# Which 32 KB block of DRAM each SBUF partition holds: a map of 32 x 4 blocks, and the last store in one piece

## Chip, cores, metric

One core of one Trainium2 chip. The metric is device time in microseconds (us). Faster or slower needs 2%; smaller differences are given with their 95% interval.

## The reference

Rotary position embedding on x of shape [16, 512, 1024], float32, with 16 heads of 64 and tables cos and sin of [512, 32]:

```python
x = x.reshape(batch, seq, num_heads, head_dim)
x1, x2 = x[..., :half_dim], x[..., half_dim:]
cos = cos[None, :, None, :]
sin = sin[None, :, None, :]
rotated = np.concatenate([x1 * cos - x2 * sin, x1 * sin + x2 * cos], axis=-1)
```

33.55 MB go in and 33.55 MB come out; everything else is small.

## The kernel before

The tensor is cut into 8 slabs of 4 MB (two batch entries each). A slab is 128 blocks of 32 KB, 8 rows of 1024 floats each, and partition p holds block p. Loads are issued by SyncE, stores by ScalarE; five slab buffers go round, and a load waits for the store that frees its buffer.

```python
    def dram(t, s, a=0, n=W):
        return bass.AP(tensor=t.tensor, offset=t.offset + s * nb * seq * dim + a,
                       ap=[[W, P], [1, n]])
    ...
    def load(s):
        slab[s] = slabs.tile([P, W], f32, tag="slab", name="slab")
        return nc.sync.dma_start(out=slab[s], in_=dram(x, s))
```

The tables arrive in one layout (partition p: sequence positions 4p to 4p+3) and are spread to the slab's layout by matmuls with a 0/1 matrix `pick`, which GpSimd builds:

```python
    for g in range(2 * G):
        part = view(pick, g * P, (SP, P // SP), (1, SP))
        nc.gpsimd.affine_select(
            out=part, in_=part, compare_op=mybir.AluOpType.not_equal,
            fill=1.0 if g < G else -1.0, base=-(g % G),
            pattern=[[0, P // SP], [-G, SP]], channel_multiplier=1)
```

Each slab is cast to bfloat16 on ScalarE, goes through two multiplies and one add on VectorE, is cast back on ScalarE and stored. The last slab is handled and stored in two halves:

```python
        back = nc.scalar.copy(out=xs, in_=xu)
        if s == nslabs - 1:
            ...  # keep the second half's cast behind the first half's store
            part = nc.scalar.dma_start(
                out=dram(out_flat, s, r * dim, n * dim), in_=xs)
        elif r + n == rpp:
            nc.scalar.dma_start(out=dram(out_flat, s), in_=slab[s])
            if s + slots < nslabs:
                load(s + slots)
```

## Time and profile before

| | before |
|---|---|
| median of 4 runs | 162.49 us (162.31 to 162.63) |
| span of the profiled run | 160.4 us |
| VectorE, ScalarE busy | 108.5 us, 113.5 us |
| the two DMA queues' share of 16 engines | 49.4% + 48.5% |
| 32 KB packet, median | 1.213 us |

How to read it: the busiest compute engine works 71% of the time and the DMA engines nearly all of it. The prediction below shows these lines and works with them. It also uses single packet records, which no view of the profile prints: start, duration, size and queue of each DMA packet. They do not say which of the 16 engines moved it; so what is said of single engines is inferred. Two things read from them: the **first byte** (start of the first load packet, 1.77 us before) and the **tail** (from the last completion packet to the end of the span, 1.45 us before).

### The profile page before, as it was taken

The page shows a single profiled execution, that of the slowest core. Times are in us where ns is not written, and L with a number is a line of the kernel's source. Part 1 is how long each engine was busy: PE and PEld are TensorE (multiplying, and loading weights), DVE is VectorE, ACT ScalarE, POOL GpSimd, SP SyncE. Part 2 cuts the span into 40 slices and gives each one's busy share as a digit, 9 for nine tenths or more (in the row PEclk, how much of TensorE's full clock was granted, in tenths as well). Part 3 has the DMA queues.
Part 4 walks back from the last instruction along what each step waited for, and adds up shares of the span by engine and source line. Part 5 has one row for each costly group of instructions (what it writes and reads, how often), then busy time and mean ns, then how long its engine had stood idle before and what let it go on. Part 6 is the DMA issues. An engine that isn't in the chain of part 4 may idle for free.

```text
span 160.4 us, 169 instructions
## 1 busy us (share of the span) xinstructions
PE 1.0 (1%) x8; PEld 0.8 (1%) x8; DVE 108.5 (68%) x34; ACT 113.5 (71%) x23; POOL 3.4 (2%) x12
## 2 busy tenths in 40 slices
PE   0011000000000000000000000000000000000000
PEld 0010000000000000000000000000000000000000
DVE  0003799999989979997996099939649599920000
ACT  3006939998998999899907997099995999471000
POOL 7000000000000000000000000000000000000000
DMA  7999999999999999999999999999999999999994
GB/s 229 441 409 400 474 433 392 449 466 392 392 392 449 466 392 425 490 392 409 490 409 409 482 417 392 490 425 392 458 458 392 433 482 392 417 490 400 400 437 208
DMA packets 2512, 67.24 MB, mean 419 GB/s; under 512 B 304, under 2 KB 304, under 8 KB 336
## 3 DMA queue, kind: packets, MB, share of 16 engines
q1 hardware_dynamic: 1152, 33.55, 49.4%
q10 hardware_dynamic: 1296, 33.56, 48.5%
q0 software_dynamic: 64, 0.13, 0.2%
HBM read 33.69 MB, written 33.55 MB: 419 GB/s over the span
## 4 chain that ended last, share of the span: by engine, by line
DMA 59%; ACT 17%; issue 9%; DVE 4%; SPq 0%; POOLq 0%
DMA slab<-in_x_dram 40%; DMA out_dram<-slab 15%; ACT slab L146 11%; ACT xb L119 6%; DMA raw<-in_cos_dram 4%; DVE xb L143 1%; DVE xb L140 1%; DVE slab L140 1%; SPq L62 0%; POOLq L177 0%
## 5 line engine op out<-in xcount | busy, mean ns | idle before, releaser
L119 ACT CAST xb<-slab 128x4096 bf16<-128x4096 f32 (+1 forms) x11 | 56.6, 5155 | 27.4 <-DMA slab<-in_x_dram 26.1
L146 ACT CAST slab<-xb 128x4096 f32<-128x4096 bf16 (+1 forms) x11 | 56.6, 5153 | 3.4 <-DVE xb L143 3.4
L140 DVE TENSOR_TENSOR slab<-xb,tab 128x4096 bf16<-128x4096 bf16 (+1 forms) x11 | 35.9, 3260 | 19.7 <-ACT xb L119 19.6
L143 DVE TENSOR_TENSOR xb<-xb,slab 128x4096 bf16<-128x4096 bf16 (+1 forms) x11 | 35.9, 3261 | 0.3
L140 DVE TENSOR_TENSOR xb<-xb,tab 128x4096 bf16<-128x4096 bf16 (+1 forms) x11 | 35.9, 3260 | 0.3
L110 DVE CAST tab<-acc 128x1024 bf16<-128x1024 f32 x1 | 1.2, 1225 | 12.6 <-PE acc L104 12.6
L119 ACT ACT_TABLE_LOAD x1 | 1.3, 1283 | 0.7 <-PEq L177 0.7
L104 PE MATMUL acc<-tab,pick 128*128 128x128 bf16 x8 | 1.0, 305 | 11.6 <-POOL tab L98 11.6
L92 POOL TENSOR_SCALAR_AFFINE_SELECT pick<-pick 128x128 bf16<-128x128 bf16 x4 | 1.0, 289 | 0.1
L104 PEld LDWEIGHTS <-pick 128*128 128x128 bf16 x8 | 0.8, 136 | 11.4 <-issue 8.1
L73 POOL DMA_DIRECT2D raw<-in_cos_dram x1 | 0.7, 677 | 0.8 <-POOLq L177 0.8
L98 POOL CAST tab<-raw 128x256 bf16<-128x256 f32 x1 | 0.4, 398 | 7.0 <-DMA raw<-in_sin_dram 7.0
L89 POOL MEMSET pick<- 128x512 bf16 x1 | 0.5, 544 | 0.0
L73 POOL DMA_DIRECT2D raw<-in_sin_dram x1 | 0.5, 537 | 0.0
L177 POOL MEMSET const-float32-0.0<- 128x1 f32 x1 | 0.1, 99 | 0.2 <-issue 0.2
L177 POOL MEMSET const-bfloat16-1.0<- 128x1 bf16 x1 | 0.1, 102 | 0.0
L177 POOL MEMSET const-uint8-127<- 128x1 uint8 x1 | 0.1, 102 | 0.0
L177 POOL MEMSET const-float32-1.0<- 128x1 f32 x1 | 0.1, 99 | 0.0
## 6 DMA issues: line engine op xcount, KB each, us to landing
slab<-in_x_dram SPq DMA_DIRECT2D x8, 4096.0 KB, 24.6
out_dram<-slab ACTq DMA_DIRECT2D x7, 4096.0 KB, 27.8
out_dram<-slab ACTq DMA_DIRECT2D x2, 2048.0 KB, 15.3
raw<-in_cos_dram POOLq DMA_DIRECT2D x1, 64.0 KB, 7.1
raw<-in_sin_dram POOLq DMA_DIRECT2D x1, 64.0 KB, 9.1
```

The source lines that it names most:

```text
L73: table[i] = nc.gpsimd.dma_start(out=view(raw, i * TR * half, (1, TR * half)), in_=bass.AP(tensor=src.tensor, offset=src.offset, ap=[[TR * ...
L89: nc.gpsimd.memset(pick, 0.0)
L92: nc.gpsimd.affine_select(out=part, in_=part, compare_op=mybir.AluOpType.not_equal, fill=1.0 if g < G else -1.0, base=-(g % G), pattern=[[ ...
L98: nc.gpsimd.tensor_copy(out=tab1, in_=raw)
L104: nc.tensor.matmul(view(acc, (i * rpp + g * TR) * hd + h * half, (hd, TR), (1, half)), view(pick, (i * h * G + g) * P, (1, P)), view(tab1, ...
L110: nc.vector.tensor_copy(out=tab, in_=acc)
L119: nc.scalar.copy(out=view(xb[s], r * dim, (1, n * dim)), in_=view(slab[s], r * dim, (1, n * dim)))
L140: nc.vector.tensor_mul(out=t, in0=xu, in1=view(tab, a + r * hd, (hd, n), (0, nh), (1, hd)))
L143: nc.vector.tensor_add(out=xu, in0=xu, in1=view(t2, half, (hd, n * nh), (-half, 2), (1, half)))
L146: back = nc.scalar.copy(out=xs, in_=xu)
L177: nc = _bacc.Bacc("TRN2", target_bir_lowering=False, num_devices=1)
```

## The change

Partition 4i+j now holds block i+32j, where it held block 4i+j, so the DRAM side of a transfer is a pattern of 32 x 4 blocks where it was 128 plain rows. The intent was that the DMA engines work on neighbouring 32 KB blocks at any one time. The `pick` matrices follow the new map, and the last slab is stored whole.

```diff
-    def dram(t, s, a=0, n=W):
-        return bass.AP(tensor=t.tensor, offset=t.offset + s * nb * seq * dim + a,
-                       ap=[[W, P], [1, n]])
+    PJ = P // 4
+
+    def dram(t, s):
+        return bass.AP(tensor=t.tensor, offset=t.offset + s * nb * seq * dim,
+                       ap=[[W, PJ], [PJ * W, 4], [1, W]])
...
-        part = view(pick, g * P, (SP, P // SP), (1, SP))
+        part = view(pick, g * P, (4, PJ), (2, 2), (1, 2))
...
-            pattern=[[0, P // SP], [-G, SP]], channel_multiplier=1)
+            pattern=[[-G, PJ], [0, 2], [-G * PJ, 2]], channel_multiplier=1)
...
-        back = nc.scalar.copy(out=xs, in_=xu)
-        if s == nslabs - 1:
-            ...
-            part = nc.scalar.dma_start(
-                out=dram(out_flat, s, r * dim, n * dim), in_=xs)
-        elif r + n == rpp:
+        nc.scalar.copy(out=xs, in_=xu)
+        if r + n == rpp:
             nc.scalar.dma_start(out=dram(out_flat, s), in_=slab[s])
```

More of the change, by code (lines that the diff above doesn't have):

```diff
@@ L34 @@
     W = rpp * dim
-    SP = seq // rpp
     TW = rpp * half
@@ L144 @@
             out=xu, in0=xu, in1=view(t2, half, (hd, n * nh), (-half, 2), (1, half)))
-        back = nc.scalar.copy(out=xs, in_=xu)
-        if s == nslabs - 1:
-            if r > 0:
-                tc.add_manual_dep(
-                    back.ins, part.ins.name,
-                    mybir.DependencyInfo(mybir.DependencyClass.NoSync,
-                                         mybir.DependencyReason.DATA),
-                    reason="issue")
-            part = nc.scalar.dma_start(
-                out=dram(out_flat, s, r * dim, n * dim), in_=xs)
-        elif r + n == rpp:
+        nc.scalar.copy(out=xs, in_=xu)
+        if r + n == rpp:
             nc.scalar.dma_start(out=dram(out_flat, s), in_=slab[s])
```

## The prediction

Passages are cut, and marked. The sum was -0.1 for the map, -0.07 for the last store and +0.1 for the first issue, put as about -0.1 us, 162.4 us. The first was my guess at what the map might save of the 1.5 us per engine (0.72 + 0.66 + 0.1) that slow packets take beyond 1.213 us, and rival A's 161.0 takes off that same 1.5. The +0.1 is a guess too. That packets would be twice as long in rival B I assumed. The chances are my own estimates.

> **What bounds the kernel now.** I read the page from its top first: which engine is full, then the rate of the transfers slice by slice, then the packets of each queue.
>
> ```profile
> span 160.4 us, 169 instructions
> PE 1.0 (1%) x8; PEld 0.8 (1%) x8; DVE 108.5 (68%) x34; ACT 113.5 (71%) x23; POOL 3.4 (2%) x12
> ...
> DMA  7999999999999999999999999999999999999994
> GB/s 229 441 409 400 474 433 392 449 466 392 392 392 449 466 392 425 490 392 409 490 409 409 482 417 392 490 425 392 458 458 392 433 482 392 417 490 400 400 437 208
> DMA packets 2512, 67.24 MB, mean 419 GB/s; under 512 B 304, under 2 KB 304, under 8 KB 336
> ...
> q1 hardware_dynamic: 1152, 33.55, 49.4%
> q10 hardware_dynamic: 1296, 33.56, 48.5%
> ```
>
> No compute engine is above 71%, and the row of DMA digits has no gap: every slice but the first and last is at 90% or more, and the two queues (loads on q1, stores on q10) take 49.4 + 48.5 = 97.9% of the 16 engines' time. The 1152 packets of q1 are 8 transfers of 144, that is 128 blocks of 32 KB and 16 small completion packets; q10 has 9 transfers of 144. The swing from 392 to 490 within the GB/s row is packets falling into one 4 us slice or the next; so I next asked for longer stretches (columns: stretch, its length, busy time of the engines, granted clock, DMA share, GB/s).
>
> ```profile
> 8.00:158.00 150.00, 1.01 (x8) 0.74 (x7) 108.49 (x34) 112.26 (x22) 0.40 (x1) 1.00 1.00 429
> 145.10:158.00 12.90, 0.00 (x0) 0.00 (x0) 0.00 (x0) 0.00 (x1) 0.00 (x0) 1.00 1.01 432
> ```
>
> Over 150 us the engines are busy with share 1.00 and move 429 GB/s, and the last 13 us, stores alone, move 432. Loads mixed with stores cost hardly anything against that.
>
> Last I read the trace's records of single packets, which no view prints. Of the 1,024 load packets of 32 KB the median is 1,213 ns and the fastest 1,211; all 896 store packets of 32 KB take 1,213; the 256 packets of 16 KB of the last slab take 611. So a packet goes at 32,768 B / 1,213 ns = 27.0 GB/s, and 16 engines at 432 GB/s. Only two bursts are slow[...]: the first 16 packets of all (at 1.8 to 2.6 us, 1.5 to 2.3 us each) and 16 load packets at 40.3 to 40.9 us, as the first store joins (1.6 to 2.1 us each).
>
> That gives the whole time of one engine: 128 blocks x 1.213 = 155.3 us; the first burst is 11.5 us too long over 16 engines, 0.72 each; the second 10.6, 0.66 each; some 400 load packets between 10 and 40 us are about 4 ns long, 0.1; the tables 2 packets x 0.159 = 0.3; completions 0.15; halving the last slab's packets, 16 x 0.611 - 8 x 1.213 = 0.07. Sum 157.3. The records give 157.3 us busy per engine, between a first byte at 1.77 us and a last at 158.97. After it come 1.46 us to the end of the span, 160.4, and the profiled execution was 162.2.
>
> The queue's own waits and the end of the timeline say what the issues wait for:
>
> ```profile
> SPq L62 <- DMA out_dram<-slab: 87.8, 3, 51.1
> ...
> 131.01 0.34 ACTq L158 DMA_DIRECT2D out_dram<-slab  x1
> ...
> 138.12 0.34 ACTq L155 DMA_DIRECT2D out_dram<-slab  x1
> ...
> 141.50 3.60 ACT L146 CAST slab<-xb 128x4096 f32<-128x4096 bf16 x1 [3.40 <-DVE xb L143]
> 145.13 0.34 ACTq L155 DMA_DIRECT2D out_dram<-slab  x1
> ```
>
> The last three loads wait for stores to free a slab, which looks like a dependency bound; but the engines never run dry meanwhile, so the wait costs nothing. At 145.13, when the last half is issued, (158.97 - 145.13) x 432 GB/s = 5.98 MB are still to go, while the last slab is 4.19 MB. Some 1.8 MB of the store before it are thus still ahead.
>
> [...]
>
> [...]
>
> [...]
>
> [...]
>
> **The change part by part.**
>
> 1. The map of blocks. Partition 4i+j holds block i+32j instead of block 4i+j. [...]64 loads and 64 stores of 32 KB per engine. At 1.213 us that is the same 155.3 us. [...]I book 0.1 us of gain for this.
>
> 2. The pick matrices for the tables. Still 4 affine selects over 128 x 128 (289 ns each, 1.0 us in all, finished at 4.1 us), with a three-dimensional pattern. They have slack until 11.1 us, when the tables are on the chip. Cost on the path: 0, even if each took three times as long.
>
> 3. The last store whole. The comparison of the instruction streams shows TensorE, VectorE, GpSimd and the loads in the same order; ScalarE has one store instead of two at the end. Removed: one issue of 0.34 us at 138.12, and 16 completion packets; 16 packets of 611 ns per engine become 8 of 1,213. Gain 0.07 us. Given up: the first half can't start at 138.12. But the previous store is being moved until 145.1 + 1.8 MB / 432 GB/s = 149.3 us. The whole store is issued at some 144.8 to 145.1; the first load needed 1.0 us from issue (0.74) to first byte (1.77). So it is in the queue 3 us before its turn. Cost 0. The cast of the last half also no longer waits behind a DMA issue.
>
> 4. The issue itself. A pattern of 32 x 4 blocks might take a little longer to issue than the 0.34 us now. The loads but the first, and all stores, are issued with work queued ahead; a tenth of a microsecond on the first load is all that shows.
>
> Sum: -0.1 - 0.07 + 0.1 = about -0.1 on 162.57, from which I take 162.4.
>
> **The rivals.**
>
> Rival A, DRAM conflicts are hidden in the 1,213 ns too, so that neighbouring blocks go quicker. Against it: loads and stores have the same 1,213 ns, to a few nanoseconds, alone and mixed; half the bytes take 611[...]At most the slow packets go: 162.5 - 1.5 = 161.0.
>
> Rival B, the split over the engines follows the DRAM pattern's 32 x 4[...]. With packets twice as long this goes to 160.4 + 155 = about 315 us[...]. I give this 6%.
>
> Rival C, the whole last store empties the engines at the end. It would need the backlog at 145 us to be gone; then about 4.9 us (2.1 MB at 432 GB/s) would be exposed, 167 us. The backlog of 1.8 MB speaks against it: 2%.
>
> Rival D, closer streams disturb each other in DRAM[...], lengthening packets by a few per cent. At +3% on half the packets, 2.3 us: 165 us. [...]3% for enough of it to show.
>
> **Range and chances.** The kernel is at the transfer floor, 155.3 us, plus 1.8 at the head, 1.5 at the tail and 1.8 outside the span: 160.4 in all, even with no slow packet and no other cost. A gain of over 2% means below 159.3, which is under that floor; it needs packets shorter than any in the trace: 1%. Slower by over 2% (165.8) takes B, C or a strong D: 8%. The rest, 91%, is the same. Repeats of the kernel before spread over 162.4 to 162.63; allowing for other burst lengths and 0.3% between executions, the range is 161.3 to 163.2.
>
> **What would show it right or wrong.** Right: both queues with 1,152 packets, the share of each within 1% of the span of now, 429 GB/s in the middle, load and store packets at 1,213 ns, the two bursts still there, and the last store issued near 145 us and landing near 159 to 160. Rival A shows as shorter packets or vanished bursts, B as packets of some 2.4 us and 200 to 300 GB/s, C as a drop in the DMA digits in the slices 36 to 38, D as load packets scattered above 1,213. I would be wrong on the main point if any ordinary packet took less than 1.2 us.

## The result, and the profile after

162.70 us median of 4 runs (162.61 to 162.80) against 162.49 (162.31 to 162.63): the same. The ratio is 1.0016, with an interval of 1.0001 to 1.0030.

The page of the changed kernel: span, the DMA rows by slice and the queues.

```profile
span 160.9 us, 169 instructions
...
DMA  5999999999999999999999999999999999999994
...
DMA packets 2368, 67.24 MB, mean 418 GB/s; under 512 B 288, under 2 KB 288, under 8 KB 320
...
q1 hardware_dynamic: 1152, 33.55, 49.4%
q10 hardware_dynamic: 1152, 33.55, 48.3%
```

The loads' queue is as it was, to the packet. The stores' queue lost 144 packets: one transfer fewer and no 16 KB packets. The digits are 9 from the second slice to the last but one. Only the first slice differs: 5, where it was 7.

Long stretches of the changed kernel (columns: stretch, its length, busy time of the engines, granted clock, DMA share, GB/s):

```profile
8.00:158.00 150.00, 1.01 (x8) 0.74 (x7) 108.49 (x34) 112.27 (x22) 0.40 (x1) 1.00 1.00 428
```

428 GB/s against 429: the rate did not move. Of the packet records, load and store packets have a median of 1.213 us, as before, although the map is another. The two slow bursts are still there: 14 packets of 1.78 to 2.04 us from 2.1 us on, and 30 of 1.33 to 2.30 us from 39.5 to 41.2 us.

What did move is in the first two microseconds. The first issue, in the timeline of before and then of the changed kernel (columns: start, duration):

```profile
0.74 0.37 SPq L62 DMA_DIRECT2D slab<-in_x_dram  x1
```

```profile
0.73 0.60 SPq L65 DMA_DIRECT2D slab<-in_x_dram  x1
```

All eight loads, in the answer for that line of each kernel (duration in ns, least, median and most):

```profile
L62 SPq DMA_DIRECT2D slab<-in_x_dram x8: 327/350/463, 0.7 to 98.8; - x8
```

```profile
L65 SPq DMA_DIRECT2D slab<-in_x_dram x8: 534/566/613, 0.7 to 99.5; - x8
```

The 32 x 4 pattern takes some 0.2 us more to issue, at each load (566 ns against 350, medians) and store (547 against 338). The first one has nothing queued ahead of it: its first byte comes at 2.12 us instead of 1.77. Of these 0.35 us, 0.23 is the longer issue itself; the other 0.12 passes between the end of the issue and the first byte, and no run takes it apart.

GpSimd's part also grew. The affine selects, in the group lists before and after:

```profile
L92 POOL TENSOR_SCALAR_AFFINE_SELECT pick<-pick 128x128 bf16<-128x128 bf16 x4 | 1.0, 289 | 0.1
```

```profile
L96 POOL TENSOR_SCALAR_AFFINE_SELECT pick<-pick 128x128 bf16<-128x128 bf16 x4 | 3.4, 874 | 0.1
```

They take three times as long, 874 ns. TensorE's first weight load waits for the first of them until 4.0 us instead of 3.4, which costs nothing: GpSimd's next work, and the matmuls after it, still wait for the tables (columns: what waited for what, us in total, times, longest).

```profile
POOL tab L102 <- DMA raw<-in_sin_dram: 4.8, 1, 4.8
```

Before, that wait was 7.0 us: the slower selects have used up slack.

The end of the changed kernel's timeline:

```profile
142.40 3.60 ACT L150 CAST slab<-xb 128x4096 f32<-128x4096 bf16 x1 [3.46 <-DVE xb L147]
146.04 0.55 ACTq L152 DMA_DIRECT2D out_dram<-slab  x1
```

The whole last store is issued at 146.04, about 0.9 us later than the second half was before, since all that comes before it is later by about as much. The engines are busy until the last byte at 159.70.

### The profile page after: what moved, and what is told of

It is laid out like the page before. It is cut to its first block, busy times and chain, and to the rows that moved or that the text cites. A ratio compares the mean times of both kernels' runs of the same rounds, so it can differ in the third digit from the quotient of the medians. Undisturbed runs are those within 1.5% of the kernel's fastest.

```text
span 160.9 us, 169 instructions
## 1 busy us (share of the span) xinstructions
PE 1.0 (1%) x8; PEld 0.8 (1%) x8; DVE 108.5 (67%) x34; ACT 113.5 (71%) x23; POOL 5.7 (4%) x12
## 4 chain that ended last, share of the span: by engine, by line
DMA 59%; ACT 17%; issue 9%; DVE 4%; SPq 0%; ACTq 0%; POOLq 0%
DMA slab<-in_x_dram 40%; DMA out_dram<-slab 15%; ACT slab L150 11%; ACT xb L123 6%; DMA raw<-in_cos_dram 4%; DVE xb L147 1%; DVE xb L144 1%; DVE slab L144 1%; SPq L65 0%; ACTq L150 0%; POOLq L171 0%
## 5 line engine op out<-in xcount | busy, mean ns | idle before, releaser
L96 POOL TENSOR_SCALAR_AFFINE_SELECT pick<-pick 128x128 bf16<-128x128 bf16 x4 | 3.4, 874 | 0.1
```

The lines of the kernel that those rows point to most:

```text
L96: nc.gpsimd.affine_select(out=part, in_=part, compare_op=mybir.AluOpType.not_equal, fill=1.0 if g < G else -1.0, base=-(g % G), pattern=[[ ...
```

## The experiments

Two theories of why the time stays. **Floor**: the DMA engines move 32 KB per 1.213 us whatever the addresses, from first byte to last, so only the head, the tail and the number of packets can change the time. **Rival A**: DRAM spacing matters, and something else hides its gain or loss. Below that, the small difference of +0.16% had to be split among the map, the issue and the last store. The runs were made in three calls of four; the kernels of a call share their runs of the kernel before, with medians of 162.59 us (first four experiments: pattern form, whole last store, map, first load plain), 162.48 (transfers alone, rows 256 KB apart, 16 x 8, 8 x 16) and 162.38 (the other four). So the same median can have two ratios. The medians of the table are over all runs; the ratios leave slow runs out (one of six with the first load plain; three of four at 16 x 8; two of four at 8 x 16 and at 16 x 8 with groups apart).

| run | median, us | ratio to before | interval |
|---|---|---|---|
| pattern form only | 162.82 | 1.0012 | 0.9998 to 1.0025 |
| whole last store only | 162.13 | 0.9972 | 0.9959 to 0.9986 |
| map only | 163.01 | 1.0031 | 1.0017 to 1.0046 |
| changed kernel, first load plain | 162.21 | 0.9978 | 0.9962 to 0.9993 |
| transfers alone | 161.89 | 0.9960 | 0.9941 to 0.9980 |
| rows 256 KB apart | 162.82 | 1.0018 | 1.0000 to 1.0035 |
| 16 x 8 form | 237.17 | none: scattered 214 to 251 | |
| 8 x 16 form | 407.07 | 2.4759 | 2.4633 to 2.4884 |
| 16 x 8 form, groups 256 KB apart | 232.57 | 1.4186 | 1.4156 to 1.4216 |
| whole last store, slab 3 in halves | 162.41 | 1.0001 | 0.9989 to 1.0014 |
| 64 x 2 form | 162.77 | 1.0023 | 1.0008 to 1.0038 |
| changed kernel again | 162.82 | 1.0025 | 1.0012 to 1.0038 |

### Is it the transfers, and do the addresses matter?

**Transfers alone.** From the kernel before, all arithmetic on the slabs is taken out (a wrong result):

```diff
-    cast(passes[0])
-    for i, (s, r, n) in enumerate(passes):
-        ...   # casts, multiplies, adds, stores
+    for s in range(nslabs):
+        nc.scalar.dma_start(out=dram(out_flat, s), in_=slab[s])
+        if s + slots < nslabs:
+            load(s + slots)
```

> Wrong result on purpose: the kernel before with all casts, multiplies and adds taken away; each slab is loaded and stored as it is, the last one whole, with the same row form and the same five slabs. Theory: the DMA engines bound the kernel from first byte to last (157.3 us busy of a 157.2 us window before), so taking away 222 us of work on two engines changes nearly nothing: 161.0 to 162.6, packets of 1.213 us, 427 to 432 GB/s. Rival: the waits of the last three loads for stores and the late start of the stores (37 us) cost time: under 158.

Measured 161.89 us. Its span and its long stretch:

```profile
span 160.2 us, 101 instructions
...
8.00:158.00 150.00, 1.01 (x8) 0.74 (x7) 1.23 (x1) 0.40 (x1) 1.00 1.00 430
```

With VectorE down to 1.2 us and ScalarE with no slab work, the time falls by 0.4% and not to under 158 us; most of the 0.4% is the whole last store (below). The late start of the stores and the waits that the arithmetic causes cost nothing that can be had back. This is the floor theory's strongest result.

**Rows 256 KB apart.** The kernel before, with slab s made of every eighth block of the whole tensor, so 256 KB from partition to partition instead of 32 KB (wrong result):

```diff
-        return bass.AP(tensor=t.tensor, offset=t.offset + s * nb * seq * dim + a,
-                       ap=[[W, P], [1, n]])
+        return bass.AP(tensor=t.tensor, offset=t.offset + s * W + a,
+                       ap=[[nslabs * W, P], [1, n]])
```

> Wrong result on purpose (the tables no longer fit the rows): slab s holds every eighth 32 KB block of the whole tensor, so that rows are 256 KB apart[...], in the plain 128-row form. Theory: addresses don't matter[...]: 162.3 to 163.0, packets of 1.213 us. Rival A or D (spacing matters, and the change goes some of the way from far to near): packets over 1.25 us and 165 us or more.

Measured 162.82 us, and in the long stretch:

```profile
8.00:158.00 150.00, 1.01 (x8) 0.74 (x7) 108.50 (x34) 112.26 (x22) 0.40 (x1) 1.00 1.00 428
```

The median packet is 1.213 us again. With 32 KB from partition to partition, 256 KB, and the map of the changed kernel (1 MB within a group of four, 32 KB from group to group) there is no difference to speak of: 429, 428 and 428 GB/s; rival A as forecast, 165 us or more, is out. An effect of a few tenths is not excluded (interval 1.0000 to 1.0035): the load packets together were 0.3 us per engine longer than in the profile of before.

### What the small difference is made of

**Map only.** The changed kernel, with the last slab stored in two halves as before:

```diff
-    def dram(t, s):
+    def dram(t, s, a=0, n=W):
...   # offset + a, and [1, n] for [1, W]
-        nc.scalar.copy(out=xs, in_=xu)
-        if r + n == rpp:
+        back = nc.scalar.copy(out=xs, in_=xu)
+        if s == nslabs - 1:
+            ...   # the two half stores of before
+        elif r + n == rpp:
```

> The changed kernel with the last slab stored in two halves as before: the new map alone. Theory F: the same time as the changed kernel, 162.6 to 162.9, ratio 1.001 to 1.002, first byte near 2.1 us. If the whole last store is what costs (rival C): 162.4 to 162.6.

Measured 163.01 us, ratio 1.0031; first byte at 2.12 us, tail 1.45. The map alone costs 0.3%, a little more than I expected, and the whole last store must give some back.

**Whole last store only.** The kernel before, with the special case of the last slab removed:

```diff
-        back = nc.scalar.copy(out=xs, in_=xu)
-        if s == nslabs - 1:
-            ...
-        elif r + n == rpp:
+        nc.scalar.copy(out=xs, in_=xu)
+        if r + n == rpp:
```

> The kernel before with the last slab stored whole and nothing else changed. Theory: no cost and no gain, 162.4 to 162.6, ratio 0.999 to 1.0005; store packets all of 1.213 us; no gap before the last store. Rival C (the late start of the last store costs something): the residual 0.2 us or more appears here, ratio 1.001 or more.

Measured 162.13 us, ratio 0.9972: outside my expectation, and on the good side. I had looked for a cost of lateness and there is a gain. The first byte is at 1.74 us and the rate the same, but the tail is 1.22 us instead of 1.45. SyncE's own waits show why. First the kernel before, then this one (columns: what waited for what, us in total, times, longest):

```profile
SPq L191 <- DMA out_dram<-slab: 35.4, 1, 35.4
```

```profile
SPq L181 <- DMA out_dram<-slab: 36.0, 4, 9.6
```

These lines are the closing code, in which SyncE waits for all transfers, one semaphore after another. Transfers of slabs share eight semaphores (in the trace of before, 17 transfers count seven semaphores up to 32 and one, that of the last half, up to 48). Before, the second half of the last slab has the one that is among the first awaited: SyncE stands 35.4 us at that wait, and after it four more waits that were long satisfied still have to be executed; in the trace the first of them starts at 159.38 and the step after the last at 159.63, some 63 ns each. With one store fewer, the last store has the semaphore that is awaited last, and the other waits are done while the data still moves. That is 0.24 us of tail (1.454 less 1.218).

**Whole last store, slab 3 in halves.** This gives the last store the early semaphore back, without touching when it is issued:

```diff
-            nc.scalar.dma_start(out=dram(out_flat, s), in_=slab[s])
+            if s == 3:
+                for a in (0, W // 2):
+                    nc.scalar.dma_start(out=dram(out_flat, s, a, W // 2),
+                                        in_=view(slab[s], a, (1, W // 2)))
+            else:
+                nc.scalar.dma_start(out=dram(out_flat, s), in_=slab[s])
```

(on top of the whole last store)

> The kernel before with the last slab stored whole and slab 3 stored in two halves instead: as many transfers and packets as before, and the last store again gets the semaphore that the closing code waits for first, with four more waits behind it. Theory C1 (what the whole last store saves is the closing chain and a few short packets, not anything about lateness): from the last completion packet to the end of the span 1.45 us as before, instead of 1.22; time 162.3 to 162.6, ratio 0.999 to 1.000. Rival C2 (storing the last slab at once saves time by itself): 162.0 to 162.25, ratio 0.997 to 0.9985, 1.22 us at the end.

Measured 162.41 us, ratio 1.0001, tail 1.45 us, and the wait is one long one again:

```profile
SPq L186 <- DMA out_dram<-slab: 41.8, 1, 41.8
```

So the gain is not from storing the last slab at once. Together with the 0.07 us of the short packets, the closing chain makes 0.3 us; the difference between this run and the one before it is 0.29% of 162.4, 0.47 us, with intervals of about 0.2 us on each. The direction and the tail are settled, the rest of the size is within the noise.

**Pattern form only.** Is it the form of the pattern or the addresses that costs? A 32 x 4 form whose groups stay 128 KB apart, with the four blocks of a group from four slabs (wrong result):

```diff
-        return bass.AP(tensor=t.tensor, offset=t.offset + s * nb * seq * dim + a,
-                       ap=[[W, P], [1, n]])
+        return bass.AP(tensor=t.tensor, offset=t.offset + (s % 4 + s // 4 * 4 * P) * W + a,
+                       ap=[[4 * W, P // 4], [P * W, 4], [1, n]])
```

> Wrong result on purpose: every transfer has the 32 x 4 form of the changed kernel, but the 32 groups stay 4 blocks (128 KB) apart, as before; the four blocks of a group come from four slabs. The last slab is stored in two halves as before. Theory F (the form costs, the addresses don't): each issue takes about 0.55 us instead of 0.35, the first byte comes near 2.1 us instead of 1.77, and the time is about that of the changed kernel, 162.6 to 162.9, ratio 1.001 to 1.002. Rival A (the addresses cost): 162.4 to 162.6, ratio under 1.0005, in spite of any longer issue.

Measured 162.82 us, ratio 1.0012 (0.9998 to 1.0025); first byte at 2.12 us, tail 1.45. Its first issue:

```profile
0.73 0.60 SPq L62 DMA_DIRECT2D slab<-in_x_dram  x1
```

The issue is exactly as long and the first byte as late as with the real map, so both belong to the form. The ratio leans the same way but its interval includes 1, so by the time alone this run would be inconclusive.

**First load plain.** The changed kernel, with the 128-row form for the very first load (slab 0 is wrong):

```diff
-        return nc.sync.dma_start(out=slab[s], in_=dram(x, s))
+        return nc.sync.dma_start(out=slab[s], in_=dram(x, s) if s else bass.AP(
+            tensor=x.tensor, offset=x.offset, ap=[[W, P], [1, W]]))
```

> Wrong result on purpose: the changed kernel, but the first load alone has the plain 128-row form of before. Theory F says that only the first issue of all is on the path (0.2 us longer in the changed kernel, first byte 0.35 us later): first byte back near 1.8 us and the time down by 0.2 to 0.35 us against the changed kernel, 162.3 to 162.6, ratio 0.999 to 1.0005. If the cost lies in later packets (addresses, the longer burst at 40 us): still 162.6 to 162.9, ratio 1.001 to 1.002.

Measured 162.21 us, ratio 0.9978, first byte at 1.75 us, tail 1.23. (One of its six runs took 164.53 us and counts as slow; the ratio leaves it out, and the median of the other five is 162.10.) The time is below the range I expected, 0.999 to 1.0005: the ratio is 0.38 to 0.47% under the changed kernel's two (1.0016 and 1.0025), about twice the 0.2 to 0.35 us forecast. The seven other loads and all stores keep the slower issue at no cost that can be seen. The ratio is that of the whole last store alone, 0.9972: with the first load plain, the map costs nothing that can be measured.

**The changed kernel again**:

> The changed kernel once more, beside the others of this call. Sum of the parts: +0.37 us (first byte later) - 0.24 us (closing chain) - 0.07 us (no packets of 16 KB) = +0.06 us, plus up to 0.2 us of longer bursts: 162.5 to 162.8, ratio 1.000 to 1.002; first byte at 2.12 us and 1.22 us from the last completion packet to the end.

Measured 162.82 us, ratio 1.0025: just over the upper end of the expected ratio. First byte at 2.12, tail 1.22, as expected. The measured parts sum to +0.37 (2.12 less 1.74 to 1.77 in the kernels with a plain first load) - 0.24 - 0.07 = +0.06 us. The measured difference is 0.26 us in the first comparison and 0.41 in this one, with intervals down to 0.02 and 0.19. So some 0.2 to 0.35 us remain; at the lower ends of the intervals, nothing or 0.13 us. The two single changes, map +0.31% and last store -0.28%, together give +0.03%, 0.05 us, with intervals of 0.14% on each, so part of the remainder may be noise. In the single profiles the window from first byte to last is 157.5 to 157.9 us in the five profiles where the first load has the 32 x 4 or 64 x 2 form, against 157.2 to 157.4 in the five where it has the plain form at the old spacing (157.7 in the plain one with rows 256 KB apart), and part of that is longer load packets. Why a slower first issue should lengthen what follows is not settled. That the first load causes it is only indicated, by the run above, and by the packet records: what the packets over 1.25 us after the first burst take beyond 1.213 us adds up to 0.66 to 0.77 us per engine in the five kernels with a plain first load at the old spacing, and to 0.89 to 1.27 in the five with the 32 x 4 or 64 x 2 form. But it is 1.20 in the plain one with rows 256 KB apart, so the form of the first load is not the only thing that lengthens it.

### Could the form of the pattern have gone wrong? The prediction's rival B

**16 x 8 form.** The changed kernel with groups of eight:

```diff
-    PJ = P // 4
+    PJ = P // 8
-                       ap=[[W, PJ], [PJ * W, 4], [1, W]])
+                       ap=[[W, PJ], [PJ * W, 8], [1, W]])
```

(`pick` stays as the changed kernel has it, so the result is wrong; the next two forms the same.)

> Wrong result on purpose (the tables are those of the changed kernel): partition 8i+j holds block i+16j, a DRAM form of 16 x 8 blocks instead of 32 x 4. If the split over the engines goes by SBUF partitions whatever the DRAM form, the time is that of the changed kernel, 162.5 to 163.0, packets of 1.213 us on 16 engines. If it follows the DRAM form (prediction's rival B),[...] packets take up to 2.4 us: 180 us or more.

Measured 237.17 us median, from 214.46 to 251.06. The first part of the fastest run, with loads alone:

```profile
0.00:8.00 8.00, 0.00 (x0) 0.10 (x1) 0.00 (x0) 1.28 (x1) 5.33 (x11) 1.00 0.91 197
8.00:35.00 27.00, 1.01 (x8) 0.74 (x7) 8.99 (x5) 7.11 (x2) 0.40 (x1) 1.00 1.02 215
```

The share is that of 16 busy engines, and they move 215 GB/s: half. The same 27 us of the kernel before:

```profile
8.00:35.00 27.00, 1.01 (x8) 0.74 (x7) 19.06 (x9) 18.97 (x5) 0.40 (x1) 1.00 1.00 430
```

The packets of the first 35 us have a median of 2.55 us, twice 1.213. From 100 to 160 us, with loads and stores mixed, they are back at 1.213, and at the end, with stores alone, many take over 2 us again. Why they recover while both directions run is not settled.

**16 x 8 form, groups apart.** Is it groups on neighbouring blocks that are slow?

```diff
-        return bass.AP(tensor=t.tensor, offset=t.offset + s * nb * seq * dim,
-                       ap=[[W, PJ], [PJ * W, 4], [1, W]])
+        return bass.AP(tensor=t.tensor, offset=t.offset + s * W,
+                       ap=[[8 * W, P // 8], [P * W, 8], [1, W]])
```

> Wrong result on purpose: the 16 x 8 form again, but with the 16 groups 8 blocks (256 KB) apart in DRAM instead of side by side. Theory P ([...]whatever the DRAM addresses): as slow as the near 16 x 8 form, 205 to 255 us, load packets of 2.4 to 2.57 us while loads are alone. Rival A (neighbouring DRAM blocks on all 16 engines are what was slow there): 162.5 to 163.2 us, packets of 1.213 us.

Measured 232.57 us, 230.06 to 250.76; the profile fell on a run of the slower kind. Loads alone:

```profile
8.00:35.00 27.00, 1.01 (x8) 0.74 (x7) 8.47 (x5) 7.11 (x2) 0.40 (x1) 1.00 0.99 208
```

Load packets have a median of 2.55 us again. Neighbouring blocks are out as the cause. The eight blocks of a group lie 4 MB apart here, but so do the four of a group in "pattern form only", which took 162.82 us, so this step alone is not the cause either: it is the form. What in the form halves the rate was not shown, since no record names an engine.

**64 x 2 form**, `PJ = P // 2` and a second dimension of 2. The figures are for the case that every form with at least 32 groups runs at full speed; otherwise I expected packets over 1.3 us and 180 us or more:

> Wrong result on purpose (the tables are those of the changed kernel): partition 2i+j holds block i+64j, a DRAM form of 64 x 2 blocks. [...]162.5 to 163.0 us, packets of 1.213 us.[...]

Measured 162.77 us, 1.0023, and 428 GB/s over the 150 us: as good as 32 x 4. Loads alone:

```profile
8.00:35.00 27.00, 1.01 (x8) 0.74 (x7) 18.91 (x8) 18.80 (x5) 0.40 (x1) 1.00 1.00 432
```

The slow-down comes with fewer than 32 groups, of those tried: loads alone moved 431 GB/s at 32 x 4 and 432 here, but 215 and 208 with 16 groups.

**8 x 16 form**, `PJ = P // 16` and a second dimension of 16:

> Wrong result on purpose: partition 16i+j holds block i+8j, a DRAM form of 8 x 16 blocks. [...]only 8 engines work, at 27 GB/s each: about 2 x 157.3 + 5 = 320 us, DMA share 0.5, 8 completion packets per transfer, so 136 packets each instead of 144. If the number of engines doesn't depend on the DRAM form: 162.5 to 163.0 and 144 packets.

Measured 407.07 us (400.88 to 411.94; the ratio in the table is that of its two faster runs), more than the 320 expected. The page of a slow run (408.4 us):

```profile
DMA  5444444455444454555455455445544554454431
GB/s 112 106 103 103 103 103 103 103 122 109 154 196 215 215 209 209 221 215 170 186 221 215 186 218 212 212 193 218 215 209 196 218 135 122 128 154 144 167 128 39
...
q1 hardware_dynamic: 1088, 33.55, 26.4%
q10 hardware_dynamic: 1088, 33.55, 22.3%
```

1088 is 8 x 136, so eight completion packets per transfer where it was 16, and the DMA share is 0.50 over 150 us, which agrees with half of the engines busy, as forecast. In the middle they reach 215 GB/s, eight times 27. In the first quarter, loads alone, it is 103, and the load packets have a median of 2.55 us as at 16 x 8: a slow-down of the same kind comes on top, and that is what my 320 us left out.

## Why the prediction was right, point by point

- **The bound** was right. Taking all slab arithmetic away leaves 161.89 us, and the packets stay at 1.213 us in every kernel with 32 or more groups. So was the range: 162.70 lies in 161.3 to 163.2.
- **Part 1, the map**: right that the packets would not change; the booked 0.1 us of gain was not there. The bursts remained, the second one spread over more packets (30 over 1.25 us instead of 16); but the kernels with the old map and the last store whole, or with slab 3 in halves, have 26 and 32, so the spread alone is no sign of the map. What causes the bursts no run shows. The "some 400" packets that are slightly long are 320, longer by 5.2 ns on average; the 0.1 us that came of it stands.
- **Part 2, the pick matrices**: right, and the margin was needed: "even if each took three times as long" is what happened, 874 ns for 289, at no cost.
- **Part 3, the last store whole**: lateness costs nothing, as forecast, though the issue came at 146.0 us, a microsecond later than I had put it, and the last completion packet at 159.7. The term "Gain 0.07 us" was mis-sized: the place of the last semaphore in the closing chain adds 0.23 us, which I had not looked at. I had taken the 1.46 us after the last byte as a constant.
- **Part 4, the issue**: the right place, but "a tenth of a microsecond on the first load" was 0.35 us at the first byte.
- **The sum** of -0.1 us thus had the wrong sign: measured +0.26 us, of which +0.06 us is accounted for by terms, the rest is open as said above. (Its terms give -0.07, so 162.5 and not the 162.4 taken from them.) That the number came so close is partly luck: the first byte was put 0.25 us too low and the 0.23 us of the closing chain were not seen at all, and the two nearly cancel.
- **Rival B** was rightly called unlikely for 32 x 4, and what it forecast is real: one factor of two further, at 16 x 8, packets take 2.55 us and the time is 32% longer or more. What halves the rate there was not shown. Rivals A, C and D did not show.

## What to carry to other kernels

Here nearly all single DMA packets took the same shortest time, 1.213 us, and none of the arrangements of addresses tried with 32 or more groups shortened it; what was left was the number of bytes, the first byte and the closing waits. The outer dimension of a DRAM pattern is not mere notation: keep it at 32 or more here (or plainly 128), for with loads alone 16 ran at half the rate (215 GB/s against 430) and 8 at a quarter (109, at a DMA share of 0.51). Give the very first load the pattern that issues fastest (first byte at 1.75 us instead of 2.12), and look at which transfer's semaphore the program awaits last: the kernel before with only its last store made whole ran 0.28% under the kernel before, and is the fastest full kernel of this study.
